# Even layer of a hybrid decoder: gates projected as [column, token], values of two heads per weight unit, softmax denominators and value copies through DRAM

## The chip, the cores and the metric

The kernel runs on one core of a Trainium2 chip. The time is device microseconds (us) of one execution; the median of several runs is the figure compared. The engines are named as in the profile: PE (TensorE matmul), PEld (its weight loads), DVE (VectorE), ACT (ScalarE), POOL (GpSimd) and SP (SyncE, which here only issues DMAs; all DMAs of this kernel are issued by SP, on one queue).

## The reference

A decoder trunk of two layers on x of 1024 tokens by 1024 channels: `h = h + even_mixer(norm(h))`, `h = h + odd_mixer(norm(h))`, then a final norm. The change touches only the even layer:

```python
def even_mixer(hn, w_in, w_out, lb, hgrn_norm_w):
    aq, ak, av, ag, bq, bf, bi, bg = split(hn @ w_in, [1024] * 8)
    a_out = dilated_mixture_attention(aq, ak, av)     # 16 heads of 64, windows (128,1) (512,4) (2048,16)
    b_out = hgrn2_chunked(bq, bf, bi, lb, hgrn_norm_w)  # 8 heads of 128, gated linear recurrence, RMS norm per head
    mixed = concatenate([a_out * silu(ag), b_out * silu(bg)], axis=-1)
    return mixed @ w_out
```

Each of the eight slices of the input projection has 1024 columns. `av` and `bi` are the values of the two head groups, `ag` and `bg` their gates. The attention output of a head is a sum over three dilated windows divided by one common denominator per token and head; the kernel multiplies the sum by the reciprocal of that denominator and by silu of the gate.

## The kernel before, in words

Matrix products are float32 products split into a high and a low part, three matmuls each (`mm3`, lines 147 to 151, so lines 148, 149 and 150 in the profile). The weights of the input projection come in units of 256 columns by 1024 rows, 4 DMAs of 256 KB each (`raww`); ACT rounds each piece to the high part (`w_hi`, line 113) and DVE subtracts for the low part (`w_lo`, line 114). One unit is loaded ahead (`unit`, line 136).

A unit is used in one of two ways:

- `proj_cols` (line 226) takes 128 of its columns as the stationary operand and streams 512 tokens: output [column, token], two halves of 8 x 3 matmuls of 512.
- `proj_toks` (line 241) takes 128 tokens as the stationary operand and streams the unit's 256 columns: output [token, column], eight blocks of 8 x 3 matmuls of 256.

Both are generators that hand back control after 6 matmuls of 512 or 12 of 256, each step counted as 1.3; `mix` (line 153) takes such steps as filling between the pieces of another generator.

Stage 1 (HGRN): for each of 8 heads `hgrn_chain(b)` runs, filled with the projections of the next head, `hgrn_in(b + 1)`: q and f by `proj_cols` (names bq, bf), then value and gate together by `proj_toks` (bi). Near the end of the chain POOL multiplies gate, norm and output (lines 524, 525), PE transposes the output (bt, line 531), ACT writes it to `y` and SP stores it to `ymix` in DRAM.

Stage 2 (attention): for each of 8 pairs of heads (called p) `attn(p)` runs, filled with `attn_in(p + 1)`: value and gate by `proj_toks` (av), q and k by `proj_cols` (aq, ak). PE's order is the written one here; ACT's, POOL's and SP's orders, and DVE's, are set by the planner. In `attn(p)`, eight blocks of 128 queries: `scores` (lines 587, 592) into two PSUM banks of tag "a" (there are two), DVE adds the window counts and takes the maximum (596), ACT takes exponents and sums the denominator `den` (601), `turn` lets DVE transpose 32x32 blocks into `PB` (607), and `near` and `distant` (621, 633) multiply with the values. Queries are held in the order (c a): partition 32a + c holds token 4c + a of its block. The values are needed replicated over the four residues a: `blocks` (557) copies them from SBUF to SBUF, 16 DMAs of 64 KB for half the tokens (`V<-v`, 564), and 4 of 96 KB for the far keys (`VF<-v`, 571).

The denominators go back to token order in `weigh` (636): 4 small DMAs, a reciprocal on DVE, and POOL multiplies the gate by it (645). `write` (647) transposes the weighed gate on PE (`gt`, 8 transposes into two banks "a", line 653), ACT halves it into `y`, DVE multiplies with the attention sums (657) and SP stores `y`. Both are called in the next head's `attn`: `weigh(p - 1)` after the scores of block 0, `write(p - 1)` in block 1. The last two blocks' products of head p - 1 (`rest`) are also done there.

Stage 3: in `attn(7)` the fill is the first four groups of the output projection, `out_first(range(4))` (names op, hres), with y read back from `ymix` (`rawy`, cut by the same lines 113 and 114 into yphi and yplo). In this part DVE's order is the written one too. The residual tiles `hres` take buffers of the tags X0, X1, v and sg.

Of the kernel before, what the change touches and what calls it, by code (L numbers as in the profile page):

```python
# [19 lines left out]
P = 128  # L20
# [16 lines left out]
C_LV = C_MA + 128  # L37
C_ID32 = C_LV + 5 * 16
C_T0 = C_ID32 + 32
C_ALL = C_T0 + 512  # L40


def const_table():
    c = np.zeros((P, C_ALL), np.float32)
    p = np.arange(P)
    c[:, C_ID:C_ID + 128] = np.eye(P)

    a, q = p // 32, p % 32 * 4 + p // 32

    def count(dist):  # L50
        cnt = np.zeros(dist.shape, np.int64)
        for window, dil in ((128, 1), (512, 4), (2048, 16)):
# [12 lines left out]
    for lv in range(5):  # L65
        s = 1 << lv
        blk = j // s
        i = np.arange(32)
        odd = i[(i // s) % 2 == 1]
        c[:, C_LV + 16 * lv:C_LV + 16 * lv + 16] = (blk[:, None] % 2 == 0) & (blk[:, None] + 1 == odd[None, :] // s)  # L70
    c[:, C_ID32:C_ID32 + 32] = j[:, None] == np.arange(32)[None, :]

    i, j = np.arange(32)[:, None], np.arange(16)[None, :]
    for par in range(2):
        c[(p // 16) % 2 == par, C_T0:C_T0 + 512] = (i == 2 * j + par).reshape(-1)
    return c


@with_exitstack
def trunk_kernel(ctx: ExitStack, tc: tile.TileContext, x, ew, ewo, ow, owab, owo, nw, fnw, lbl, hnw,  # L80
# [11 lines left out]
    def bank(tag, shape, name):  # L92
        return pp.tile(shape, F32, name=name, tag=tag, bufs=BANKS[tag])
# [226 lines left out]
    def even_layer(es):  # L320
        ep = es.enter_context(tc.tile_pool(name="ev", bufs=2))
        sm = es.enter_context(tc.tile_pool(name="evs", bufs=2))

        BIGS = {"X0": 2, "X1": 2, "v": 2, "sg": 3, "y": 2}
        HGS = {"q": 2, "f": 2, "AT": 2, "tot": 2, "osb": 2, "kn": 1, "S": 1, "nwb": 1, "x": 2}
        WAY = {"nwb": 1, "yh": 2, "yl": 2, "xn": 2, "h4": 1, "h5": 1, "h6": 1, "h7": 1}
        pool_of = {}
# [59 lines left out]
        nc.sync.dma_start(id32, cst[:, C_ID32:C_ID32 + 32])  # L387
        hw = sm.tile([P, 1], F32, name="hw", bufs=1)
        nc.sync.dma_start(hw, hnw)
        def hgrn_in(b):  # L390
            w = unit()
# [10 lines left out]
            for half in range(2):  # L402
                yield from proj_cols(w, 0, f"bq{b}", lambda s, ps: act.copy(q[:, s], ps), (half,))
                yield from proj_cols(w, 1, f"bf{b}", ev_f, (half,))
            dve.tensor_scalar(f, f, lb1[:, b:b + 1], lb[:, b:b + 1], op0=ALU.mult, op1=ALU.add)
            dve.tensor_scalar(kt, kt, lb1[:, b:b + 1], None, op0=ALU.mult)
            dve.tensor_tensor(qt, q, f, op=ALU.mult)
            w = unit()
            v = big("v", f"bv{b}", (P, NT, 128))
            sg = big("sg", f"bsg{b}", (P, NT, 128))  # L410
            INS[b] += [v, sg]

            def ev_v(t, ps):
                act.copy(v[:, t, :], ps[:, 0:128])
                act.activation(sg[:, t, :], ps[:, 128:256], AF.Sigmoid)
                dve.tensor_tensor(sg[:, t, :], ps[:, 128:256], sg[:, t, :], op=ALU.mult)

            yield from proj_toks(w, f"bi{b}", ev_v)

        INS = {}  # L420

        def hgrn_chain(b):
            q, qt, kt, f, v, sg = INS[b]
# [97 lines left out]
            act.activation(sd, ss, AF.Sqrt, bias=epsc, scale=1.0 / 128)  # L521
            rs = sm.tile([P, NT], F32, name=f"brs{b}", tag="brs")
            dve.reciprocal(rs, sd)
            pool.tensor_tensor(sg, sg, rs[:, :, None].to_broadcast([P, NT, 128]), op=ALU.mult)
            pool.tensor_tensor(osb, osb, sg, op=ALU.mult)
            yield 7.0
            y = big("y", f"by{b}")
            for h in range(2):
                tp = bank("d", [P, 512], f"bt{b}_{h}")
                for c in range(4):  # L530
                    pe.transpose(tp[:, c * 128:(c + 1) * 128], osb[:, 4 * h + c, :], ident)
                act.activation(y[:, h * 512:h * 512 + 512], tp, AF.Copy, scale=hw)
            nc.sync.dma_start(ymix[D + b * 128:D + (b + 1) * 128, :], y)

        def attn_in(p):
            w = unit()
            v = big("v", f"v{p}", (P, NT, 128))  # L540
            sg = big("sg", f"sg{p}", (P, NT, 128))
            INS[p] = [v, sg]

            def ev_v(t, ps):
                dve.tensor_copy(v[:, t, :], ps[:, 0:128])
                th = sm.tile([P, 128], F32, name=f"th{p}_{t}", tag="th")
                act.activation(th, ps[:, 128:256], AF.Tanh, scale=0.5)
                dve.scalar_tensor_tensor(sg[:, t, :], th, 1.0, ps[:, 128:256], op0=ALU.add, op1=ALU.mult)

            yield from proj_toks(w, f"av{p}", ev_v)  # L550
            w = unit()
            q, k = big("X0", f"aq{p}"), big("X1", f"ak{p}")
            INS[p] += [q, k]
            yield from proj_cols(w, 0, f"aq{p}", lambda s, ps: act.copy(q[:, s], ps))
            yield from proj_cols(w, 1, f"ak{p}", lambda s, ps: dve.tensor_copy(k[:, s], ps))

        def blocks(p, h):

            v = INS[p][0]

            V4 = at.tile([P, 4, NT // 2, 128], F32, name=f"V4{h}_{p}", tag=f"V4{h}")
            for b in range(4):
                for a in range(4):
                    nc.sync.dma_start(V4[32 * a:32 * a + 32, b], v[32 * b:32 * b + 32, NT // 2 * h:NT // 2 * h + NT // 2, :])
            VB.setdefault(p, []).append(V4)
            if h:

                VF = at.tile([P, NFAR, 128], F32, name=f"VF{p}", tag="VF")
                vr = v.rearrange("(c a) t d -> a c t d", a=4)
                for a in range(4):  # L570
                    nc.sync.dma_start(VF[32 * a:32 * a + 32], vr[a, :, 0:NFAR, :])
                VB[p].append(VF)

        def scores(p, i, den):

            q, k = INS[p][2:]
# [58 lines left out]

        def weigh(p):

            sg, den = INS[p][1], DEN[p]
            rd = sm.tile([P, NT, 2], F32, name=f"rd{p}", tag="rd")
            rv = rd.rearrange("(c a) t e -> a c t e", a=4)  # L640
            for a in range(4):
                nc.sync.dma_start(rv[a], den[32 * a:32 * a + 32])
            dve.reciprocal(rd, rd)
            g = sg.rearrange("p t (e d) -> p t e d", e=2)
            pool.tensor_tensor(g, g, rd[:, :, :, None].to_broadcast([P, NT, 2, 64]), op=ALU.mult)

        def write(p):
            sg, o = INS[p][1], O[p]
            y = big("y", f"ay{p}")
            for h in range(2):  # L650
                tp = bank("a", [P, 512], f"gt{p}_{h}")
                for t in range(4):
                    pe.transpose(tp[:, t * 128:(t + 1) * 128], sg[:, 4 * h + t, :], ident)
# [5 lines left out]

        def attn(p):  # L660

            DEN[p] = den = sm.tile([P, NT, 2], F32, name=f"den{p}", tag="den")
            if not p:
                blocks(0, 0)
            for i in range(NT):
                if i == 2:
# [22 lines left out]
        DEN, O, VB = {}, {}, {}  # L689


        h, h2, ready, asked = [], [], [4, 5, 6, 7, 0, 1, 2, 3], set()
# [42 lines left out]
        at = open_stage("at")  # L735
        G = at.tile([P, WG], F32, name="G")
        nc.sync.dma_start(G, cst[:, C_G:C_G + WG])
        PB = at.tile([P, 2, NT * WG + 192], F32, name="PB")
        with tc.manual_schedule(engines={mybir.EngineType.PE}):
            for p in range(7):  # L740
# [495 lines left out]
def host_layout(a):  # L1236
# [4 lines left out]
    for s in r128:  # L1241
        cols += [[np.r_[2048 + s, 3072 + s]], [s, 1024 + s]]
    for s in r128:
        cols += [[4096 + s, 5120 + s], [np.r_[6144 + s, 7168 + s]]]

    def unit(w, c):

# [51 lines left out]
```

## Time and profile before

| | |
|---|---|
| median of 3 runs | 2289.87 us (2287.13 to 2292.92) |
| the profiled execution, time | 2288.19 us |
| its span in the profile | 2286.4 us, 54636 instructions |
| granted TensorE clock, mean | 0.992 |
| PE busy | 2168.5 us, 95% of the span |
| DVE, ACT, POOL busy | 1427.2, 963.2, 227.7 us |
| first and last score matmul of the attention | 547.3 and 1051.7 us |

A row of the timeline gives the start in us from the span's start, the duration, the engine, the line of the kernel, the operation, what it writes and reads, shapes and a count; in square brackets stands the engine's idle time before it and what ended it. Rows of one kind that follow each other are merged with the count behind the x. PE overlaps its matmuls, so the pace of a stream is the distance between starts, not the duration.

### The profile page before, as it was taken

What the parts mean: (1) busy time and instruction counts of PE and PEld (TensorE: products, weight loads), DVE (VectorE), ACT (ScalarE), POOL (GpSimd) and SP (SyncE); (2) the same over time, 40 slices, a digit from 0 to 9 for tenths busy, and PEclk for the clock granted to TensorE, in tenths of its full rate; (3) what the DMA queues carried; (4) which work ended last, traced back from release to release, by engine and by line L of the source; (5) the groups of instructions that cost most, each with busy time, mean ns of one, the idle gap of its engine ahead of it and who ended that gap; (6) DMA issues with size and microseconds to landing.
All of it is one profiled execution on the core that took longest, in us unless ns stands there. A gap on an engine that the chain in (4) does not pass through costs nothing. (4 is left out here: it accounts for less than half of the span.)

```text
span 2286.4 us, 54636 instructions
## 1 busy us (share of the span) xinstructions
PE 2168.5 (95%) x22597; PEld 1806.7 (79%) x22597; DVE 1427.2 (62%) x3364; ACT 963.2 (42%) x2623; POOL 227.7 (10%) x236
## 2 busy tenths in 40 slices
PE   7999999999999999979999988989998989899998
PEld 6888888898888888857887776767777767678787
DVE  6444444444444444456677887878788877855777
ACT  5333333333323332322236663755555555544223
POOL 0000000000000000000000012131212121210000
PEclk9999999999999999989999999999999999999999
DMA  4111111113222323342234221121212121214232
GB/s 145 38 48 48 48 44 48 43 39 95 79 80 83 90 83 92 97 150 86 90 121 106 60 56 61 53 79 45 77 42 77 51 75 59 65 61 148 92 112 110
DMA packets 101864, 175.83 MB, mean 77 GB/s; under 512 B 16752, under 2 KB 34032, under 8 KB 101616
## 3 DMA queue, kind: packets, MB, share of 16 engines
q1 hardware_dynamic: 101616, 172.35, 24.3%
q8 instruction: 177, 2.90, 0.5%
q14 instruction: 71, 0.58, 0.1%
HBM read 127.07 MB, written 25.23 MB: 67 GB/s over the span
## 5 line engine op out<-in xcount | busy, mean ns | idle before, releaser
L114 DVE TENSOR_TENSOR w_lo<-raww,w_hi 128x512 fp32r<-128x512 f32 x292 | 212.1, 727 | 147.6 <-ACT w_hi L113 144.7
L113 ACT CAST w_hi<-raww 128x512 fp32r<-128x512 f32 x292 | 181.0, 620 | 265.7 <-DMA raww<-in_ewo_dram 52.7
L148 PE MATMUL av<-w_hi,hn_hi 128*128 128x256 f32 x512 | 149.1, 291 | 0.0
L148 PE MATMUL bi<-w_hi,hn_hi 128*128 128x256 f32 x512 | 147.0, 287 | 0.0
L149 PE MATMUL bi<-w_lo,hn_hi 128*128 128x256 f32 x512 | 145.4, 284 | 0.0
L150 PE MATMUL bi<-w_hi,hn_lo 128*128 128x256 f32 x512 | 144.9, 283 | 0.0
L149 PE MATMUL av<-w_lo,hn_hi 128*128 128x256 f32 x512 | 144.8, 283 | 0.0
L150 PE MATMUL av<-w_hi,hn_lo 128*128 128x256 f32 x512 | 144.6, 282 | 0.0
L601 ACT ACTIVATE P<-P,nm 128x256 f32<-128x256 f32 (+7 forms) x128 | 71.4, 559 | 130.2 <-DVE nm L599 126.8
L148 PE MATMUL op<-w_hi,yplo 128*128 128x512 f32 x288 | 113.9, 396 | 2.4 <-DVE hres L293 1.6
L150 PE MATMUL op<-w_hi,yplo 128*128 128x512 f32 x288 | 112.3, 390 | 0.0
L149 PE MATMUL op<-w_lo,yplo 128*128 128x512 f32 x288 | 112.2, 390 | 0.0
L148 PE MATMUL pv<-hn_hi,w_hi 128*128 128x512 f32 x256 | 107.2, 419 | 2.9 <-ACT uv L849 2.9
L148 PE MATMUL oz<-hn_hi,w_hi 128*128 128x512 f32 x256 | 109.3, 427 | 0.0
L293 DVE TENSOR_TENSOR hr<-hr,op 128x512 f32<-128x512 f32 x128 | 86.2, 684 | 33.7 <-PE op L150 33.5
L150 PE MATMUL pv<-hn_hi,w_lo 128*128 128x512 f32 x256 | 104.3, 408 | 0.0
L149 PE MATMUL pv<-hn_lo,w_hi 128*128 128x512 f32 x256 | 102.8, 402 | 0.0
L149 PE MATMUL oz<-hn_lo,w_hi 128*128 128x512 f32 x256 | 102.1, 399 | 0.0
L150 PE MATMUL oz<-hn_hi,w_lo 128*128 128x512 f32 x256 | 101.7, 397 | 0.0
L148 PEld LDWEIGHTS av<-w_hi,hn_hi 128*128 128x128 f32 x512 | 97.7, 191 | 3.5 <-issue 1.9
L148 PEld LDWEIGHTS bi<-w_hi,hn_hi 128*128 128x128 f32 x512 | 98.1, 192 | 0.0
L149 PEld LDWEIGHTS bi<-w_lo,hn_hi 128*128 128x128 f32 x512 | 98.1, 192 | 0.0
(354 smaller groups left out, 5994.4 us busy)
## 6 DMA issues: line engine op xcount, KB each, us to landing
raww<-in_ew_dram SPq DMA_DIRECT2D x128, 256.0 KB, 3.1
raww<-in_ow_dram SPq DMA_DIRECT2D x100, 256.0 KB, 3.0
V<-v SPq DMA_DIRECT2D x256, 64.0 KB, 2.0
rawy<-ymix SPq DMA_DIRECT2D x64, 256.0 KB, 2.7
raww<-in_ewo_dram SPq DMA_DIRECT2D x32, 256.0 KB, 3.0
gcl<-gcd SPq DMA_DIRECT2D x64, 128.0 KB, 3.0
gca<-gcd SPq DMA_DIRECT2D x64, 128.0 KB, 3.0
ymix<-oy SPq DMA_DIRECT2D x32, 256.0 KB, 2.1
```

The source lines that it names most:

```text
L113: act.copy(hi, raw)
L114: dve.tensor_tensor(lo, raw, hi.bitcast(F32), op=ALU.subtract)
L148: pe.matmul(ps, lh, rh, start=start, stop=False)
L149: pe.matmul(ps, lh, rl, start=False, stop=False)
L150: pe.matmul(ps, ll, rh, start=False, stop=stop)
L293: dve.tensor_tensor(dst[:, n], src[:, n], ps, op=ALU.add)
L601: act.activation(Pm[:, e, w0:], Pm[:, e, w0:], AF.Exp, bias=nmx[:, e:e + 1], scale=0.125, accum_out=den[:, i, e:e + 1])
```

## The change

Weights are regrouped: for two neighbouring blocks of 128 columns, s and z (two HGRN heads, or two of the attention's head pairs p), there are again four units, [v s | v z], [q s | k s], [gate s | q z], [k z | gate z] in the attention, and [q s | f s], [v s | v z], [gate s | q z], [f z | gate z] in HGRN. Values of two heads come from one `proj_toks`; gates come from `proj_cols`, so they are [column, token].

- HGRN: POOL multiplies the output by the norm before the transposes, and `y` by the gate after them.
- `blocks(p, 0)` stores the values of p to DRAM once (`vd`), and the copies are read from there, 4 DMAs in place of 16 for each half, and 4 for the far keys as before.
- The reciprocal is taken at the end of `attn(p)` on DVE. `weigh(p - 1)`, now called before the scores of block 0, brings it to token order and to rows with one matmul against a permutation matrix of halves (`PM`), into a bank "a"; ACT copies it out, SP stores it to DRAM (`rdd`) and loads it back into `y`, each row read by 64 partitions; POOL multiplies by the gate. `write` no longer transposes.
- Buffers: tag v 2 to 3, tag sg 3 to 2.

```diff
-        BIGS = {"X0": 2, "X1": 2, "v": 2, "sg": 3, "y": 2}
+        BIGS = {"X0": 2, "X1": 2, "v": 3, "sg": 2, "y": 2}
...
+        def values(b, name, copies):
+            w = unit()
+            V[b], V[b + 1] = (big("v", f"{name}{i}", (P, NT, 128)) for i in (b, b + 1))
+            def ev(t, ps):
+                for i in range(2):
+                    copies[i](V[b + i][:, t, :], ps[:, i * 128:i * 128 + 128])
+            yield from proj_toks(w, f"{name}p{b}", ev)
...
+            w = unit()
+            if b % 2 == 0:
+                for half in range(2):
+                    yield from proj_cols(w, 0, f"bq{b}", ev_q, (half,))
+                    yield from proj_cols(w, 1, f"bf{b}", ev_f, (half,))
+                rest()
+                yield from values(b, "bi", (act.copy, act.copy))
+            else:
+                yield from gate(w, 0, b - 1)
+                yield from proj_cols(w, 1, f"bq{b}", ev_q)
+                w = unit()
+                yield from proj_cols(w, 0, f"bf{b}", ev_f)
+                rest()
+                yield from gate(w, 1, b)
...
-            pool.tensor_tensor(sg, sg, rs[:, :, None].to_broadcast([P, NT, 128]), op=ALU.mult)
-            pool.tensor_tensor(osb, osb, sg, op=ALU.mult)
+            pool.tensor_tensor(osb, osb, rs[:, :, None].to_broadcast([P, NT, 128]), op=ALU.mult)
...
+                pool.tensor_tensor(y[:, h * 512:h * 512 + 512], y[:, h * 512:h * 512 + 512], SG[b][:, h * 512:h * 512 + 512],
+                                   op=ALU.mult)
...
+            if p % 2 == 0:
+                yield from values(p, "av", (dve.tensor_copy, act.copy))
+                w = unit()
+                yield from proj_cols(w, 0, f"aq{p}", ev_q)
+                yield from proj_cols(w, 1, f"ak{p}", ev_k)
+            else:
+                w = unit()
+                yield from gate(w, 0, p - 1)
+                yield from proj_cols(w, 1, f"aq{p}", ev_q)
+                w = unit()
+                yield from proj_cols(w, 0, f"ak{p}", ev_k)
+                yield from gate(w, 1, p)
...
-            for b in range(4):
-                for a in range(4):
-                    nc.sync.dma_start(V4[32 * a:32 * a + 32, b], v[32 * b:32 * b + 32, NT // 2 * h:NT // 2 * h + NT // 2, :])
+            if not h:
+                VD[p] = dp.tile([P, T], F32, name=f"vd{p}")
+                nc.sync.dma_start(VD[p], V[p].rearrange("p t d -> p (t d)"))
+            vd = VD[p]
+            for a in range(4):
+                nc.sync.dma_start(V4[32 * a:32 * a + 32].rearrange("p b t d -> p b (t d)"),
+                                  bass.AP(tensor=vd.tensor, offset=vd.offset + 512 * h, ap=[[T, 32], [32 * T, 4], [1, 512]]))
...
-            for a in range(4):
-                nc.sync.dma_start(rv[a], den[32 * a:32 * a + 32])
-            dve.reciprocal(rd, rd)
-            g = sg.rearrange("p t (e d) -> p t e d", e=2)
-            pool.tensor_tensor(g, g, rd[:, :, :, None].to_broadcast([P, NT, 2, 64]), op=ALU.mult)
+            rd = RD[p]
+            rp = bank("a", [2 * NT, 128], f"rp{p}")
+            pe.matmul(rp, rd.rearrange("p e t -> p (e t)"), PM, start=True, stop=True)
+            rs = sm.tile([2 * NT, 128], F32, name=f"rs_{p}", tag="rs_")
+            act.copy(rs, rp)
+            rdd = dp.tile([2 * NT, 128], F32, name=f"rdd{p}")
+            nc.sync.dma_start(rdd, rs)
+            y = Y[p] = big("y", f"ay{p}")
+            for e in range(2):
+                nc.sync.dma_start(y[64 * e:64 * e + 64], bass.AP(tensor=rdd.tensor, offset=rdd.offset + e * T, ap=[[0, 64], [1, T]]))
+            for h in range(2):
+                n = slice(512 * h, 512 * h + 512)
+                pool.tensor_tensor(y[:, n], y[:, n], SG[p][:, n], op=ALU.mult)
...
-            for h in range(2):
-                tp = bank("a", [P, 512], f"gt{p}_{h}")
-                for t in range(4):
-                    pe.transpose(tp[:, t * 128:(t + 1) * 128], sg[:, 4 * h + t, :], ident)
-                act.mul(y[:, h * 512:h * 512 + 512], tp, 0.5)
...
-            if not p:
+            if p:
+                weigh(p - 1)
+            else:
                 blocks(0, 0)
...
-                if i == 0 and p:
-                    weigh(p - 1)
...
+                if i == NT - 1:
+                    rd = RD[p] = sm.tile([P, 2, NT], F32, name=f"rd{p}", tag="rd")
+                    dve.reciprocal(rd.rearrange("p e t -> p t e"), den)
```

More of the change, by code (lines that the diff above doesn't have):

```diff
@@ L39 @@
 C_T0 = C_ID32 + 32
-C_ALL = C_T0 + 512
+C_PM = C_T0 + 512
+C_ALL = C_PM + 128
 def const_table():
@@ L400, in ev_f @@
                 act.activation(kt[:, s], ps, AF.Sigmoid, scale=-1.0)
[L402 to L407, printed above, removed]
@@ L408, in hgrn_in, with ev_q @@
-            w = unit()
[L409 to L420, printed above, removed]
+            def ev_q(s, ps):
+                act.copy(q[:, s], ps)
@@ new lines, in rest, with gate, ev @@
+            def rest():
+                dve.tensor_scalar(f, f, lb1[:, b:b + 1], lb[:, b:b + 1], op0=ALU.mult, op1=ALU.add)
+                dve.tensor_scalar(kt, kt, lb1[:, b:b + 1], None, op0=ALU.mult)
+                dve.tensor_tensor(qt, q, f, op=ALU.mult)
+            def gate(w, c, i):
+                sg = SG[i] = big("sg", f"bsg{i}")
+                def ev(s, ps):
+                    act.activation(sg[:, s], ps, AF.Sigmoid)
+                    dve.tensor_tensor(sg[:, s], ps, sg[:, s], op=ALU.mult)
+                yield from proj_cols(w, c, f"bg{i}", ev)
@@ L422, in hgrn_chain @@
+        INS, V, SG = {}, {}, {}
         def hgrn_chain(b):
-            q, qt, kt, f, v, sg = INS[b]
+            (q, qt, kt, f), v = INS[b], V[b]
             AT = big("AT", f"AT{b}", (P, NT, 128))
@@ L544, in ev_v @@
[L544 to L551, printed above, removed]
-            q, k = big("X0", f"aq{p}"), big("X1", f"ak{p}")
-            INS[p] += [q, k]
@@ L554, in attn_in, with ev_q, ev_k, gate @@
-            yield from proj_cols(w, 0, f"aq{p}", lambda s, ps: act.copy(q[:, s], ps))
-            yield from proj_cols(w, 1, f"ak{p}", lambda s, ps: dve.tensor_copy(k[:, s], ps))
+            q, k = big("X0", f"aq{p}"), big("X1", f"ak{p}")
+            INS[p] = [q, k]
+            def ev_q(s, ps):
+                act.copy(q[:, s], ps)
+            def ev_k(s, ps):
+                dve.tensor_copy(k[:, s], ps)
+            def gate(w, c, i):
+                sg = SG[i] = big("sg", f"sg{i}")
+                def ev(s, ps):
+                    act.activation(sg[:, s], ps, AF.Tanh, scale=0.5)
+                    dve.scalar_tensor_tensor(sg[:, s], sg[:, s], 1.0, ps, op0=ALU.add, op1=ALU.mult)
+                yield from proj_cols(w, c, f"ag{i}", ev)
@@ L636, in weigh @@
         def weigh(p):
-            sg, den = INS[p][1], DEN[p]
-            rd = sm.tile([P, NT, 2], F32, name=f"rd{p}", tag="rd")
-            rv = rd.rearrange("(c a) t e -> a c t e", a=4)
-            for a in range(4):
-                nc.sync.dma_start(rv[a], den[32 * a:32 * a + 32])
-            dve.reciprocal(rd, rd)
-            g = sg.rearrange("p t (e d) -> p t e d", e=2)
-            pool.tensor_tensor(g, g, rd[:, :, :, None].to_broadcast([P, NT, 2, 64]), op=ALU.mult)
-        def write(p):
-            sg, o = INS[p][1], O[p]
-            y = big("y", f"ay{p}")
-            for h in range(2):
-                tp = bank("a", [P, 512], f"gt{p}_{h}")
-                for t in range(4):
-                    pe.transpose(tp[:, t * 128:(t + 1) * 128], sg[:, 4 * h + t, :], ident)
-                act.mul(y[:, h * 512:h * 512 + 512], tp, 0.5)
+            rd = RD[p]
[11 more added lines that the diff above has]
+                pool.tensor_tensor(y[:, n], y[:, n], SG[p][:, n], op=ALU.mult)
+        def write(p):
+            y, o = Y[p], O[p]
             yv = y.rearrange("p (t c a) -> p a t c", c=32, a=4)
@@ L660, in attn @@
         def attn(p):
-            DEN[p] = den = sm.tile([P, NT, 2], F32, name=f"den{p}", tag="den")
-            if not p:
+            den = sm.tile([P, NT, 2], F32, name=f"den{p}", tag="den")
+            if p:
+                weigh(p - 1)
+            else:
                 blocks(0, 0)
@@ L737, in even_layer @@
         nc.sync.dma_start(G, cst[:, C_G:C_G + WG])
+        PM = at.tile([P, 128], F32, name="PM")
+        nc.sync.dma_start(PM, cst[:, C_PM:C_PM + 128])
         PB = at.tile([P, 2, NT * WG + 192], F32, name="PB")
@@ L1240, in host_layout @@
     cols = []
[L1241 to L1244, printed above, removed]
+    for s, z in zip(r128[::2], r128[1::2]):
+        cols += [[np.r_[2048 + s, 2048 + z]], [s, 1024 + s], [3072 + s, z], [1024 + z, 3072 + z]]
+    for s, z in zip(r128[::2], r128[1::2]):
+        cols += [[4096 + s, 5120 + s], [np.r_[6144 + s, 6144 + z]], [7168 + s, 4096 + z], [5120 + z, 7168 + z]]
     def unit(w, c):
```

15 lines of the change are left out of this document (5 added, 10 removed).

## The prediction

> **What bounds the kernel now.** I read the page first, then a table of windows of 60 us, then what PE waited for in each stage.
>
> ```profile
> span 2286.4 us, 54636 instructions
> PE 2168.5 (95%) x22597; PEld 1806.7 (79%) x22597; DVE 1427.2 (62%) x3364; ACT 963.2 (42%) x2623; POOL 227.7 (10%) x236
> 120.00:180.00 60.00, 59.69 (x790) 52.93 (x789) 26.07 (x56) 22.41 (x61) 5.43 (x5) 1.00 0.14 46
> 840.00:900.00 60.00, 60.00 (x1117) 51.28 (x1116) 28.64 (x78) 17.03 (x48) 1.90 (x1) 1.00 0.29 84
> 960.00:1020.00 60.00, 44.68 (x766) 34.08 (x765) 26.11 (x59) 15.46 (x38) 2.08 (x1) 0.86 0.46 144
> PE lp L451 <- DVE bkt L477: 5.1, 8, 1.6
> PE o L621 <- DVE PB L607: 11.3, 1, 11.3
> ```
>
> PE is the bound in both stages that the change touches: 59.69 of 60 us in HGRN (120 to 180), 60 of 60 in the attention (840 to 900), DVE and ACT below half. The one hole lies at 960 to 1020, where the last attention round begins: one wait of 11.3 us, and a mean clock of 0.86. In HGRN the largest wait sums to 5.1 us in 8. So only PE's own work, new waits of PE, and that hole count; evacuations, gates and POOL products lie under PE.
>
> **Projections.** Per two column blocks there were two `proj_toks` (384 matmuls of 256) and four `proj_cols` passes; now one and six: 192 matmuls of 256 are replaced by 96 of 512. Weight bytes, units and filling steps (32 a round) stay. A matmul's price is the distance of starts.
>
> ```profile
> 231.02 0.28 PE L150 MATMUL bi<-w_hi,hn_lo 128*128 128x256 f32 x1
> ...
> 238.82 0.28 PE L149 MATMUL bi<-w_lo,hn_hi 128*128 128x256 f32 x1
> ...
> 208.08 0.40 PE L150 MATMUL bq<-hn_hi,w_lo 128*128 128x512 f32 x1
> ...
> 210.14 0.39 PE L150 MATMUL bq<-hn_hi,w_lo 128*128 128x512 f32 x1
> ...
> 664.77 0.39 PE L148 MATMUL ak<-hn_hi,w_hi 128*128 128x512 f32 x1
> ...
> 668.62 0.39 PE L150 MATMUL ak<-hn_hi,w_lo 128*128 128x512 f32 x1
> ```
>
> 256 columns: 7.80 us over 65 steps, 0.120 us. 512 columns: 2.06 over 9, 0.229 us, in HGRN; 3.85 over 17, 0.2265 us, in the attention. A 512 saves 0.011 or 0.0135 us against two 256. Times 96 and four times a stage: 4.2 + 5.2 = 9.4 us less. The fence's durations (0.28 against 0.39) would promise far more, but they overlap. The Trainium skill, page "TensorE: Matmul & The Clock Gate", section "Back-to-back issue gap", gives a warm gap of N/2.4 + 2.5 ns: 109 and 216 ns, so only 2.4 ns a pair. By it this term would be an estimated 96 x 8 x 2.4 ns = 1.9 us and my sum 7.5 us smaller. The trace has 120 ns for 256, so the measurement decides.
>
> **Gate transposes.** `write` loses its 8 transposes.
>
> ```profile
> 618.93 0.28 PE L150 MATMUL av<-w_hi,hn_lo 128*128 128x256 f32 x1
> 619.05 1.04 PE L653 MATMUL gt<-ident,sg 128*128 128x128 f32 x8
> 619.84 0.36 PE L148 MATMUL av<-w_hi,hn_hi 128*128 128x256 f32 x1
> 620.04 0.28 PE L149 MATMUL av<-w_lo,hn_hi 128*128 128x256 f32 x1
> ```
>
> They hold the stream for 0.79 us, and the next matmul takes 0.20 instead of 0.12: 0.87 us a round, 8 rounds, 7.0 us less. ACT's two copies out of them go too, under PE.
>
> **The reciprocal's matmul.** It comes first in `attn(p)` for p = 1 to 7 and takes one of two banks "a"; the first score matmul takes the other, the second needs the first bank again, so PE waits until ACT has copied it out. Behind it on PE stand the scores, `rest` and all filling, so the wait counts in full. No such wait exists before; these rows bound it.
>
> ```profile
> 665.50 1.11 DVE L607 STREAM_TRANSPOSE PB<-P 128x896 f32<-128x896 f32 x1 [1.54 <-ACT P L601]
> ...
> 668.82 0.62 ACT L113 CAST w_hi<-raww 128x512 fp32r<-128x512 f32 x1 [2.10 <-PE ak L149]
> 668.94 0.48 PE L587 MATMUL S<-ak,aq 64*32 64x128 f32 x16
> ...
> 227.20 0.39 PE L512 MATMUL bops<-bv,AT 128*128 128x128 f32 x2
> ...
> 674.78 0.28 ACT L547 ACTIVATE th<-av 128x128 f32<-128x128 f32 x1 [0.69 <-DVE v L545]
> ...
> 538.03 0.60 PE L531 MATMUL bt<-ident,bo 128*128 128x128 f32 x4
> 538.66 0.69 ACT L532 ACTIVATE by<-bt,hw 128x512 f32<-128x512 f32 x1 [2.28 <-PE bt L531]
> 539.41 0.65 PE L531 MATMUL bt<-ident,bo 128*128 128x128 f32 x4
> ```
>
> The last three show such a handoff of one bank: ACT starts 0.03 us after PE's end, PE 0.06 after ACT's. Here: matmul from 668.94 (in the scores' place) for 0.39 us, ACT busy with a cast until 669.44, a copy of 128 columns 0.28, handoff 0.06: scores from 669.78, 0.84 us late. Where the filling ends with a gate (`attn_in` of odd p, ahead of four of the seven rounds) ACT first has that gate's second half, about 0.6 us more: 1.5 us. Sum 3 x 0.84 + 4 x 1.5 + 0.4 for the last `weigh` = 8.9 us more. Lower end 0.4 us each (the matmul alone), 3 us in all; upper end below, with the rivals. The reciprocal itself I take as ready: it follows `turn(7)`, which in this round ended at 666.61, 2.3 us before 668.94.
>
> **The hole at 1001.**
>
> ```profile
> 983.20 0.81 SPq L703 DMA_DIRECT2D hres<-in_x_dram  x2
> ...
> 992.07 10.74 SPq L564 DMA_DIRECT2D V<-v  x16
> 1002.91 2.44 SPq L571 DMA_DIRECT2D VF<-v  x4
> 1005.45 4.42 SPq L112 DMA_DIRECT2D rawy<-ymix  x3
> ...
> 1008.18 0.62 ACT L113 CAST yphi<-rawy 128x512 fp32r<-128x512 f32 x1 [10.01 <-DMA rawy<-ymix]
> 1011.48 0.71 DVE L607 STREAM_TRANSPOSE PB<-P 128x512 f32<-128x512 f32 x1
> 1012.24 1.29 PE L621 MATMUL o<-PB,V 32*64 32x64 f32 x64 [11.28 <-DVE PB L607]
> ...
> 986.00:988.00 2.00, 1.36 (x108) 1.22 (x109) 1.85 (x1) 0.00 (x0) 1.30 (x1) 1.00 1.00 396
> 1006.00:1008.00 2.00, 0.00 (x0) 0.00 (x0) 0.00 (x0) 0.00 (x0) 0.00 (x0) 0.50 0.75 255
> 1014.00:1016.00 2.00, 2.00 (x6) 1.55 (x5) 0.88 (x5) 0.99 (x4) 0.00 (x0) 0.50 0.33 111
> ```
>
> PE waits for `turn`, but that is DVE in written order: it stands behind the subtraction of yphi, that behind ACT's cast, that behind the load rawy, and SP issues this only after 16 V and 4 VF copies, 992.07 to 1005.35, 13.3 us. Eight DMAs replace these twenty. At 0.41 us each (hres, two in 0.81) they take 3.3 us to issue; their 1.75 MB at the 396 GB/s of 986 to 988 take 4.4 us, plus the 2.7 us that rawy took from issue to cast (1005.45 to 1008.18): a cast at 992.1 + 4.4 + 2.7 = 999.2. Against it, the store and two loads of `weigh(6)` now stand on SP ahead of it, and the residual's fourth tile takes a gate buffer that is free only after POOL's product: I allow 1 us, so 1000.2 and 8 us less idle. The clock is at 0.50 in the hole and for 3.8 us of work behind it (to 1016), which costs 1.9 us; a hole of 3 us may still lower it, so I count 1 us. Ends: 0, if SP is held elsewhere, and 11.3 + 1.9 us.
>
> **SP's waits.** Each round SP now waits for a store to DRAM before it can read it back, twice (values, reciprocals), with weight and rawy loads queued behind.
>
> ```profile
> ymix<-by SPq DMA_DIRECT2D x8, 512.0 KB, 2.6
> rawy<-ymix SPq DMA_DIRECT2D x64, 256.0 KB, 2.7
> ```
>
> A store takes 2.6 us to land, a load 2.7: about 5.3 us from copy-out to `y`, used one block later; V copies are needed some blocks later still, and weights are a unit ahead. I cost this at nothing while `attn_in` fills. If the cover is gone, each wait costs at most its 2.6 us. In the last round, where y's parts come just in time, I count 1.5 us more (0 to 5). The Trainium skill, page "DMA: Bandwidth & Descriptors", section "Anatomy of one DMA — SWDGE (gpsimd) path", puts a fixed 2.0 us on each DMA, mostly the write receipt; the trace's 2.6 us for 512 KB bears it out, and by it each readback waits about as I count.
>
> **At nothing**: HGRN's POOL products (moved behind the transposes; only the store of `y` follows), fewer and wider evacuations, the buffer counts (values of two blocks live beside one in use: three; gates of two blocks: two). Planner orders of later stages may shift by some us either way; in the range only.
>
> **Sum**: -9.4 - 7.0 + 8.9 - 8 - 1 + 1.5 = -15.0. From the profiled execution's 2288.19 us (span 2286.4 and 1.8 around it): 2273.2. That execution lay 1.7 under the median of the runs, so the median after is 2275 us.
>
> **Rivals.**
>
> 1. *The head of a round waits longer* (the slower side). If DVE does the reciprocal after the last w_lo, that waits for ACT's cast (to 669.44), so 0.7 us for w_lo, 0.25 for the reciprocal, then 0.39 + 0.28 + 0.06: 671.2, 2.2 us late, and up to 3.8 where POOL's work slows w_lo as at 533.25 (rows below this list; the reciprocal's 0.25 at 670.27). Without this term the sum is -23.9. From (23.9 - 6.9)/7 = 2.4 us a round it is no change, from (23.9 + 6.9)/7 = 4.4 us slower; at 5 us, 2290 + 11 = 2301. For it: the bank is really needed again at once. Against: `turn(7)` is long over, and the cast already waits for PE.
> 2. *The hole stays*: SP's V loads still wait, or rawy still lands late behind them. -15 + 9 = -6: 2284, no change. For it: the same loads, the same bytes, in the same place. Against: the 16 copies moved 1 MB in 10.74 us, 98 GB/s, where the same engines reached 396, so what held them was their issue.
> 3. *The paces even out*: if a stream of 512 in the new gates runs at 0.240 us, as two of 256, the 9.4 us are gone: 2284. Against: every 512 stream quoted runs at 0.23.
>
> ```profile
> 533.25 2.22 DVE L114 TENSOR_TENSOR w_lo<-raww,w_hi 128x512 fp32r<-128x512 f32 x1 [0.31 <-ACT w_hi L113]
> ...
> 670.27 0.25 DVE L643 RECIPROCAL rd<-rd 128x16 f32<-128x16 f32 x1 [2.82 <-DMA rd<-den]
> ```
>
> **How the numbers follow.** No change means within 0.3%, 6.9 us, about what a measurement of this kernel can tell. Forecast 0.62; rival 1 0.20 (0.08 of it slower, 0.12 no change); rival 2 0.14 (0.06 still faster, if half the hole closes); rival 3 0.04 (half each). Faster 0.62 + 0.06 + 0.02 = 0.70, same 0.12 + 0.08 + 0.02 = 0.22, slower 0.08. The range: all good ends (matmul alone -6, hole and clock -4, SP -1.5) give 2263; upward it takes in rival 2 and the no-change half of rival 1: 2260 to 2293. The forecast's own: 2263 to 2283.
>
> **What would show it.** Right: the distance between 512 starts stays at 0.23 and an HGRN round shrinks by 0.5 us; no gt; each round's first score matmuls 0.8 to 1.5 us later after the filling's last matmul, with PE waiting for ACT's copy; the wait before the first `near` of the last round at some 3 us. Wrong: PE waiting for the reciprocal (rival 1), an 11 us wait left (rival 2), or new waits of PE for weights or `near`'s values, which would mean that SP's readbacks are not covered.

## The result and the profile after

The changed kernel takes 2271.31 us (median of 4 runs, 2268.25 to 2272.7) against 2288.98 us before (4 runs): a ratio of 0.9919, 95% interval 0.9901 to 0.9936, so 17.7 us less, where 15 were forecast. The profiled execution took 2270.35 us, its span is 2268.6.

In what follows, a row of windows gives the window in us, its length, the busy time (and instructions) of PE, PEld, DVE, ACT and POOL, the granted clock, the time of the DMA packets as a share of 16 engines (it can exceed 1), and GB/s. A row of waits gives who waited for whom, the total in us, how often, and the longest. A row of one tile's matmuls gives their shortest, median and longest duration in ns and their first and last start.

The page of the changed kernel, the window of the table by 60 us in which the hole lay, and what PE waited for in HGRN (60 to 540 us), in the attention rounds (540 to 960) and in the last round (960 to 1080):

```profile
span 2268.6 us, 52553 instructions
PE 2162.0 (95%) x21781; PEld 1760.6 (78%) x21781; DVE 1409.7 (62%) x3236; ACT 950.0 (42%) x2551; POOL 239.5 (11%) x252
```

```profile
960.00:1020.00 60.00, 50.65 (x781) 37.97 (x780) 31.81 (x70) 16.91 (x44) 2.95 (x2) 0.89 0.52 153
```

```profile
PE lp L479 <- DVE bkt L505: 1.6, 3, 0.9
PE S L633 <- ACT rs L688: 1.3, 3, 0.4
PE op L151 <- DVE hres L296: 5.4, 3, 3.9
PE op L151 <- ACT yphi L116: 4.3, 1, 4.3
PE o L667 <- issue: 1.0, 1, 1.0
```

PE is as full as before. HGRN's wait for bkt shrank from 5.1 us in eight to 1.6 in three, which was not forecast; the rounds have the new wait for ACT's copy `rs`; and the single wait of 11.3 us is gone, but two of 4 us (hres, yphi) stand in its place.

Where the time came from can be read from three marks that both kernels have: the first score matmul, the first `near` that PE runs in the last round (it still belongs to head 6), the last score matmul. The score matmuls of the changed kernel, and the two rows of its last round's head:

```profile
L633 PE MATMUL S<-ak,aq x1024: 269/376/639, 540.0 to 1036.0; 64*32 64x256 f32 x150, 64*32 64x128 f32 x21
```

```profile
972.24 0.39 PE L686 MATMUL rp<-PM,rd 128*16 128x128 f32 x2
...
973.54 0.72 PE L667 MATMUL o<-PB,V 32*64 32x64 f32 x41
```

And the same mark of the kernel before:

```profile
983.73 0.86 PE L621 MATMUL o<-PB,V 32*64 32x64 f32 x60
```

| stretch | before | after | difference | forecast |
|---|---|---|---|---|
| to the first score (HGRN) | 547.3 | 540.0 | -7.3 | -4.2 |
| to the last round's first near | 436.4 | 433.5 | -2.9 | -1.9 |
| to the last score | 68.0 | 62.5 | -5.5 | -8.4 |
| to the end | 1234.7 | 1232.6 | -2.1 | -0.5 |

The forecast column is the prediction's own terms put to these stretches (a round's transposes at -0.87, the reciprocals' matmuls at +8.9 in all). The total came out near because two errors of some 3 us, in the first and the third stretch, had opposite signs; that is luck. Kernels with the same HGRN code (this one, and the third to seventh below) have their first score between 538.1 and 540.0, so the first stretch is known to about 1 us either way. The last stretch is known less well: these kernels, whose code there is the same, need 1232.6 to 1238.3 us for it, so its -2.1 is not clear of the spread.

### The profile page after: what moved, and what is told of

It is laid out like the page before. It is cut to its first block, busy times and chain, and to the rows that moved or that the text cites. A ratio compares the mean times of both kernels' runs of the same rounds, so it can differ in the third digit from the quotient of the medians.

```text
span 2268.6 us, 52553 instructions
## 1 busy us (share of the span) xinstructions
PE 2162.0 (95%) x21781; PEld 1760.6 (78%) x21781; DVE 1409.7 (62%) x3236; ACT 950.0 (42%) x2551; POOL 239.5 (11%) x252
## 5 line engine op out<-in xcount | busy, mean ns | idle before, releaser
L653 DVE STREAM_TRANSPOSE PB<-P 128x256 f32<-128x256 f32 (+3 forms) x64 | 54.6, 853 | 72.8 <-ACT P L647 72.8
L1156 POOL TENSOR_TENSOR gca<-gca,MA 128x256 f32<-128x256 f32 x64 | 50.6, 791 | 453.8 <-DMA gca<-gcd 252.8
L296 DVE TENSOR_TENSOR hres<-hres,op 128x512 f32<-128x512 f32 x96 | 64.7, 682 | 31.8 <-PE op L153 29.4
L642 DVE CUSTOM_DVE_ANT_0 P<-S,G 128x256 f32<-128x256 f32 (+7 forms) x128 | 58.2, 492 | 36.8 <-PE S L638 35.2
L904 DVE SCALAR_TENSOR_TENSOR vT<-uv,cws,vT 128x512 f32<-128x512 f32 x96 | 74.3, 774 | 4.7 <-ACT vT L902 3.8
L1084 DVE TENSOR_TENSOR tm<-Lp,Tp 128x126 f32<-128x126 f32 (+22 forms) x248 | 74.9, 302 | 3.7
L1158 ACT ACTIVATE gca<-gca,g_ngc 128x128 f32<-128x128 f32 x128 | 45.8, 401 | 69.3 <-POOL gca L1156 69.1
L151 PE MATMUL avp<-w_hi,hn_hi 128*128 128x256 f32 x256 | 74.5, 291 | 0.0
L151 PE MATMUL op<-w_hi,yphi 128*128 128x512 f32 x160 | 65.9, 412 | 8.5 <-ACT yphi L116 4.6
```

Of the source, the lines that this page charges most:

```text
L151: pe.matmul(ps, lh, rh, start=start, stop=False)
L296: dve.tensor_tensor(dst[:, n], src[:, n], ps, op=ALU.add)
L642: dve.tensor_tensor_reduce(Pm[:, e, w0:], S[e][:, w0:WG], G[:, w0:], 1.0, -3e38, op0=ALU.add, op1=ALU.max, accum_out=mx[:, e:e + 1])
L653: dve.transpose(PB[:, :, i * WG + w0:(i + 1) * WG], Pm[:, :, w0:])
L904: dve.scalar_tensor_tensor(a[0][:, s], ub[:, i + s.start:i + s.stop], cws[:, tile_no, i:i + 1], a[0][:, s], op0=ALU.mult, op1=ALU.add)
L1084: dve.tensor_tensor(tm[:, :31 - k, :n], Lp[:, k, k + 1:, None].to_broadcast([P, 31 - k, n]), Tp[:, k:k + 1, :n].to_broadcast([P, 31 - k, n ...
```

## The experiments

All are timed against the kernel before, which took 2290.68, 2290.26 and 2289.65 us in the three groups; ratios carry their 95% intervals.

**Each half alone.** HGRN of the change with the attention of before, and the other way round:

```diff
 # e1: hgrn_in, hgrn_chain, HGRN's unit columns from the change
-            v = big("v", f"v{p}", (P, NT, 128))
-            sg = big("sg", f"sg{p}", (P, NT, 128))
+            v = big("sg", f"v{p}", (P, NT, 128))
+            sg = big("v", f"sg{p}", (P, NT, 128))
 # e2: attn_in, blocks, weigh, write, attn, its unit columns from the change
-            v = big("v", f"bv{b}", (P, NT, 128))
-            sg = big("sg", f"bsg{b}", (P, NT, 128))
+            v = big("sg", f"bv{b}", (P, NT, 128))
+            sg = big("v", f"bsg{b}", (P, NT, 128))
```

> Only the HGRN half of the change; the attention is that of before (its value and gate tiles swap the two buffer tags, so that the tags' sizes are those of the change). Theory: the gain of HGRN stands by itself, 96 x 8 matmuls' worth of pace there (4.2 us) and 3.5 us less of PE waiting for DVE's bkt: about -7.5 us against before, 2281.5; the profile shows the wait lp <- bkt near 1.6 us in place of 5.1 and the first score matmul near 540 us in place of 547. Rival: the pace alone, -4 us (2285), the waits being a matter of the planner's order; second rival: no gain without the attention half, 2289.

> Only the attention half; HGRN is that of before (its value and gate tiles swap the two buffer tags). Theory: -10 us against before, 2279: about -4.5 in the rounds (pace -5.2, transposes gone -5.2, the reciprocal's bank wait +5.8), -5 in the last round, -1 behind it. Rival: the halves share a gain (order of later stages), then this gives clearly more or less than 17.7 minus what the HGRN half alone gives.

HGRN alone: 2282.41 us, 0.9967 (0.9955 to 0.9978), 7.6 us less. Attention alone: 2279.14 us, 0.9949 (0.9935 to 0.9962), 11.7 us less. Together 19.3, against the 18.6 that 0.9919 makes of the same base: the halves add up. PE's waits for bkt in HGRN, first of the HGRN half, then of the attention half (whose HGRN is the old one):

```profile
PE lp L476 <- DVE bkt L502: 1.3, 4, 0.4
```

```profile
PE lp L465 <- DVE bkt L491: 4.6, 8, 1.2
```

The waits for bkt go with the HGRN half and stay with the old HGRN: 3.3 to 3.8 us of shorter waits leave some 4 of the 7.6 for the pace, whose forecast was 4.2. The first score of the HGRN half comes at 539.0 us. The rival of the pace alone is out.

**The value copies.** `blocks` taken from the kernel before, all else as changed:

```diff
-            for a in range(4):
-                nc.sync.dma_start(V4[32 * a:32 * a + 32]..., bass.AP(tensor=vd.tensor, ...))
+            for b in range(4):
+                for a in range(4):
+                    nc.sync.dma_start(V4[32 * a:32 * a + 32, b], v[32 * b:32 * b + 32, NT // 2 * h:NT // 2 * h + NT // 2, :])
...
```

> The change, with the value copies taken from SBUF again (16 + 16 + 4 DMAs a round, no copy in DRAM). Theory: the twenty DMAs are what held SP and the yphi loads at the last round's start, so the 11 us wait of the first near comes back and the time is 4 to 8 us above the changed kernel, 2275 to 2279; the rounds before stay at 124.8 us a pair. Rival: what shortened the hole is the moved reciprocal and the loads' order on SP, not the copies: within 2 us of the changed kernel, 2271.

2278.36 us, 0.9939 (0.9924 to 0.9953): some 4.6 us of the gain gone by the ratios, whose intervals overlap, 7 by the medians. SP's rows, and PE's waits in the last round:

```profile
979.13 12.74 SPq L607 DMA_DIRECT2D V<-av  x16
991.97 2.45 SPq L614 DMA_DIRECT2D VF<-av  x4
994.51 1.00 SPq L115 DMA_DIRECT2D rawy<-ymix  x2
```

```profile
PE op L151 <- DVE hres L296: 11.0, 3, 9.4
PE op L151 <- ACT yphi L116: 4.8, 1, 4.8
```

The twenty copies hold SP for 15.3 us (13.3 in the kernel before), yphi's loads start at 994.5, and a wait of 9.4 us is back, in front of hres instead of near. From the first near of the last round (973.60) to the last score (1042.9) this kernel takes 69.3 us, the changed one 62.5; up to that near they agree within half a microsecond. So the copies through DRAM are worth 5 to 7 us, all of it in the last round.

**The reciprocal's bank.** One word changed:

```diff
-            rp = bank("a", [2 * NT, 128], f"rp{p}")
+            rp = bank("pj", [2 * NT, 128], f"rp{p}")
```

> The change, with the reciprocal's matmul in a projection bank (tag pj) in place of a score bank (tag a). Theory: the scores no longer wait for ACT's copy, so the gap from the matmul to the first near shrinks from 1.14 and 1.6 us to about 0.75, 3 x 0.4 + 4 x 0.85 = 4.6 us less: 2266.7 against 2271.3 for the change. Rival: the wait moves to the filling's first projection, which needs the pj bank that the last evacuation or the copy still holds: no gain, 2271.

2265.92 us, 0.9892 (0.9876 to 0.9908). Two heads of rounds in the changed kernel, one behind a gate's projection and one behind k's, then the first of them in this one:

```profile
597.36 0.39 PE L153 MATMUL ag<-hn_hi,w_lo 128*128 128x512 f32 x1
597.68 0.39 PE L686 MATMUL rp<-PM,rd 128*16 128x128 f32 x2
598.00 0.43 PE L633 MATMUL S<-ak,aq 64*32 64x128 f32 x2
598.87 0.48 PE L633 MATMUL S<-ak,aq 64*32 64x128 f32 x14 [0.43 <-ACT rs L688]
...
660.83 0.39 PE L686 MATMUL rp<-PM,rd 128*16 128x128 f32 x2
661.15 0.89 PE L633 MATMUL S<-ak,aq 64*32 64x128 f32 x16
661.97 0.85 PE L667 MATMUL o<-PB,V 32*64 32x64 f32 x60
```

```profile
595.83 0.39 PE L686 MATMUL rp<-PM,rd 128*16 128x128 f32 x2
596.15 0.48 PE L633 MATMUL S<-ak,aq 64*32 64x128 f32 x16
596.56 0.85 PE L667 MATMUL o<-PB,V 32*64 32x64 f32 x60
```

In the changed kernel two score matmuls run, the other fourteen wait for `rs`: from `rp` to the first near 1.14 us behind k (660.83 to 661.97) and, with the scores' 0.41 us added to 598.87, 1.6 us behind a gate. In the projection bank it is 0.73 (595.83 to 596.56). In the last round of the changed kernel it was 1.30 (972.24 to 973.54), so 3 x 0.41 + 3 x 0.87 + 0.57 = 4.4 us were to be had. 5.4 came by the medians (2271.31 to 2265.92); the intervals of the two ratios overlap, the rows decide for 4.4. In the rounds the wait did not move to the fill: from 540 to 950 us PE has no wait left. In the last round 0.7 us of it did (0.4 for the bank, which hres still held, 0.3 for `rs`).

**The transposes back.** Eight per round, as before, results unused:

```diff
         def write(p):
             y, o = Y[p], O[p]
+            for h in range(2):
+                tp = bank("a", [P, 512], f"gt{p}_{h}")
+                for t in range(4):
+                    pe.transpose(tp[:, t * 128:(t + 1) * 128], SG[p][:, (4 * h + t) * 128:(4 * h + t + 1) * 128], ident)
```

> The change, with 8 transposes a round put back into the score banks where they stood (their results are read by nobody). Theory: each round gets 0.87 us longer, 7.0 us in all: 2278. Rival: in the changed kernel PE has slack there (it waits for ACT or DVE anyway in each round), so they cost less than 3 us: below 2274.

2276.34 us, 0.9945 (0.9931 to 0.9959), 5.0 us above the change by the medians, 6.0 by the ratios, whose intervals overlap. The transposes and the heads of rounds 2 and 4 of this kernel:

```profile
611.50 1.04 PE L703 MATMUL gt<-ident,sg 128*128 128x128 f32 x8
...
661.28 0.39 PE L686 MATMUL rp<-PM,rd 128*16 128x128 f32 x2
...
787.97 0.39 PE L686 MATMUL rp<-PM,rd 128*16 128x128 f32 x2
```

Two rounds take 126.7 us here (787.97 - 661.28). In the changed kernel, whose fourth round has its head at 785.67, they take 124.84:

```profile
785.67 0.39 PE L686 MATMUL rp<-PM,rd 128*16 128x128 f32 x2
```

That is 0.92 us a round, against 0.87 forecast. Over all six rounds from the first head to the last (597.26 to 977.16, against 597.68 to 972.24) it is 0.89. The rival of slack in PE is out.

**What is left of the hole.** In the changed kernel the loads of SP, the two waits of PE, ACT and DVE ahead of the second wait, and windows of 2 us read:

```profile
976.95 1.09 SPq L693 DMA_DIRECT2D ay<-rdd  x2
...
979.47 2.35 SPq L609 DMA_DIRECT2D V<-vd  x4
981.92 4.68 SPq L616 DMA_DIRECT2D VF<-vd  x4
987.41 1.45 SPq L115 DMA_DIRECT2D rawy<-ymix  x2
```

```profile
983.79 0.79 PE L151 MATMUL op<-w_hi,yphi 128*128 128x512 f32 x1 [4.32 <-ACT yphi L116]
994.23 0.79 PE L151 MATMUL op<-w_hi,yphi 128*128 128x512 f32 x1 [3.85 <-DVE hres L296]
```

```profile
992.23 1.29 ACT L116 CAST yphi<-rawy 128x512 fp32r<-128x512 f32 x2 [5.13 <-DMA rawy<-ymix]
992.88 0.69 DVE L117 TENSOR_TENSOR yphi<-rawy,yphi 128x512 fp32r<-128x512 f32 x1 [6.37 <-ACT yphi L116]
993.49 0.68 DVE L296 TENSOR_TENSOR hres<-hres,op 128x512 f32<-128x512 f32 x1
```

```profile
984.00:986.00 2.00, 2.00 (x5) 1.35 (x6) 1.97 (x8) 0.00 (x0) 1.83 (x2) 0.50 1.04 194
986.00:988.00 2.00, 2.00 (x6) 1.51 (x6) 0.52 (x1) 1.09 (x4) 0.00 (x0) 0.50 1.08 231
...
998.00:1000.00 2.00, 2.00 (x89) 1.82 (x74) 2.00 (x7) 0.38 (x1) 0.00 (x0) 0.50 0.52 209
```

The eight copies leave SP in 7 us (979.47 to 986.60) where I had 3.3, and the DMA engines are full at 194 to 231 GB/s, half of the 396 that I had. The yphi loads start at 987.4, their cast comes at 992.2, and behind it stand DVE's subtraction, hres and PE. Two experiments took this apart. In one, each copy fills 128 partitions instead of 32 (with the same bytes and rows, but with other keys' rows, so the near products are wrong); in the other, on top of the projection bank, the copies are asked for two blocks later:

```diff
 # e5
-            for a in range(4):
-                nc.sync.dma_start(V4[32 * a:32 * a + 32]..., ap=[[T, 32], [32 * T, 4], [1, 512]])
+            for b in range(4):
+                nc.sync.dma_start(V4[:, b]..., ap=[[T, P], [1, 512]])
 # e6
-                if i == 1:
+                if i == (1 if p < 7 else 3):
                     blocks(p, 1)
```

> The change, with the V4 loads filling all 128 partitions each (same bytes, same size of row, same number of DMAs; each partition gets another key's row, so the near products use wrong values; only the time is of interest). The changed kernel moved 194 to 257 GB/s with its DMA engines fully busy while these loads ran, 396 was seen elsewhere. Theory: a load into only 32 partitions is what is slow; then these loads land in some 3 us instead of 5.3, the DMA share at the last round's start drops, the wait of 3.9 us behind them shrinks by 2 to 3 us, and the time is 2 to 4 us below the change, 2268 to 2269. Rival: the rate is that of reading back DRAM or of the traffic beside it; landing stays near 5 us and the time within 1 us of 2271.

> On top of the reciprocal in a projection bank: in the last round the second half of the V copies and the far keys are asked for in block 3 instead of block 1, so SP puts them behind the loads of yphi. Theory: those copies' 1.75 MB ahead of yphi are what is left of the hole; the wait of PE on hres at 990 us (3.3 us in that kernel) goes and the clock is not lowered a second time: 4 to 5 us less, 2261 to 2262 against 2265.9. Rival: the loads of the residual and of the reciprocals hold SP as well, or near then waits for its values: 0 to -1 us, 2265.

The wide rows: 2267.46 us, 0.9905 (0.9891 to 0.9918), 3.2 us under the change by the ratios, whose intervals overlap, so the times do not settle it. Two windows in a middle round, with the copies of the changed kernel and then with the wide ones:

```profile
612.00:614.00 2.00, 2.00 (x19) 2.00 (x19) 0.78 (x3) 0.27 (x1) 0.00 (x0) 1.00 1.09 240
614.00:616.00 2.00, 2.00 (x61) 1.73 (x63) 0.48 (x2) 0.27 (x1) 0.00 (x0) 1.00 1.01 254
```

```profile
610.00:612.00 2.00, 2.00 (x19) 2.00 (x19) 1.17 (x3) 0.27 (x1) 0.00 (x0) 1.00 0.98 306
612.00:614.00 2.00, 2.00 (x44) 1.75 (x42) 0.29 (x1) 0.27 (x1) 0.00 (x0) 1.00 1.02 312
```

With the engines as full, 306 to 312 GB/s in place of 240 to 254: the number of partitions is part of the rate, though not all of the distance to 396 (the far keys' loads kept their 32). The copies' median time to landing went from 5.3 to 4.0 us, where 3 was expected. The wait on hres shrank only from 3.9 to 3.1 us, not by the 2 to 3 expected, and the wait for yphi grew from 4.3 to 4.8.

The late copies: 2262.88 us, 0.9882 (0.9868 to 0.9895), 3 us under the kernel with the projection bank alone, again with overlapping intervals. Its waits in the last round:

```profile
PE op L151 <- ACT yphi L116: 3.7, 1, 3.7
...
PE op L151 <- DVE hres L296: 1.5, 2, 1.3
```

The wait behind the copies is gone (4.9 us in three to 1.5 in two), so they were its cause. The one ahead of them, 3.7 us for yphi, stays: it stands behind the reciprocals' readback and the residual's loads on SP. Those were not moved, so that they are its cause is not shown.

**The clock in the last round.** Waits are only part of what the last round costs; work at a granted clock of 0.50 is the other. For each kernel, from the first near of the last round to the last score: the time in which PE is idle, and the time lost to the clock, an estimate that takes half of PE's busy time at 0.50 (all in us of the profiled executions):

| kernel | stretch | PE idle | lost to the clock | clock at 0.50 |
|---|---|---|---|---|
| before | 68.0 | 15.3 | 4.4 | 990.4 to 993.8, 1004.1 to 1017.7 |
| changed | 62.5 | 9.2 | 6.0 | 983.1 to 989.9, 993.3 to 1000.1 |
| copies from SBUF | 69.3 | 15.2 | 6.9 | 981.6 to 988.4, 991.8 to 1008.9 |
| projection bank | 62.4 | 11.5 | 2.7 | 973.5 to 983.7 |
| wide rows | 59.0 | 9.6 | 1.6 | 980.9 to 984.4 |
| late copies, projection bank | 57.7 | 6.8 | 3.3 | 974.7 to 984.9 |

What is left of a stretch after both is 47.2 to 48.2 us in every row, so these two account for it. The change took 6.1 us from PE's idle time and lost 1.6 more to the clock. The wide rows did not shorten PE's idle time at all: their stretch is 3.5 us shorter because the clock fell once instead of twice. The late copies took 4.7 us of idle time from the kernel with the projection bank, more than the one wait of 3.3; but that kernel's clock had already fallen only once, so nothing was to be had there.

**The wide rows with the right keys**, on the change and on the fastest kernel:

```diff
-            for a in range(4):
-                nc.sync.dma_start(V4[32 * a:32 * a + 32]..., ap=[[T, 32], [32 * T, 4], [1, 512]])
+            for b in range(4):
+                nc.sync.dma_start(V4[:, b]..., bass.AP(tensor=vd.tensor, offset=vd.offset + 32 * b * T + 512 * h, ap=[[0, 4], [T, 32], [1, 512]]))
```

> The change, with each V4 load filling all 128 partitions with the right keys: one DMA for each quarter of a block, its source read four times over by a zero step outermost. Theory: as with the rows on 128 partitions before, 306 to 312 GB/s in place of 240 to 254 while such loads run, landing near 4.0 us, 3 to 4 us less than the change: 2267 to 2268. Rival, as the Trainium skill's page "DMA: Bandwidth & Descriptors", section "Rules for kernel authors", has it: an outermost dimension of 4 confines a DMA to at most 4 of the 16 engines; then each load takes about as long as four shares of it would, landing goes to 8 us or more, and the time is that of the change or above it, 2271 to 2276.

> The same loads on top of the late V copies and the reciprocal in a projection bank. Theory: where the copies already stand behind the loads of yphi their speed matters little: -0 to -2 us against 2262.9, 2261 to 2263. Rival (the four engines): 2263 to 2268.

2283.54 us, 0.9971 (0.996 to 0.9982), and 2275.96 us, 0.9939 (0.9927 to 0.9951): 12 to 13 us slower than the same kernels without it, worse than either theory had it. A window while these loads run on the change, one from the same place in the changed kernel itself, PE's longest wait with them between 530 and 950 us, which the change does not have, and its wait on hres in the last round:

```profile
546.00:548.00 2.00, 2.00 (x10) 1.64 (x9) 1.32 (x6) 0.61 (x3) 0.00 (x0) 1.00 0.26 102
```

```profile
544.00:546.00 2.00, 2.00 (x10) 1.45 (x8) 0.45 (x1) 0.12 (x2) 0.00 (x0) 1.00 1.07 218
```

```profile
PE S L633 <- DVE mx L642: 5.7, 1, 5.7
```

```profile
PE op L151 <- DVE hres L296: 12.2, 3, 10.6
```

The first wait is new, the second was 5.4: 12.5 us more, about the whole loss. The rows ahead of the first wait, which ends at 564.43:

```profile
539.36 8.84 SPq L609 DMA_DIRECT2D V<-vd  x4
552.22 3.64 SPq L115 DMA_DIRECT2D raww<-in_ew_dram  x2
562.07 0.62 ACT L116 CAST w_hi<-raww 128x512 fp32r<-128x512 f32 x1 [12.61 <-DMA raww<-in_ew_dram]
```

Four copies hold SP for 8.84 us (1.89 in the changed kernel), the weight load behind them goes out at 552.22 instead of 546.20, and ACT waits 12.6 us for it. In the order that the planner gave ACT here, this cast stands ahead of the gate and the next exponents (in the changed kernel behind them, at 563.00), so the maximum of the scores, and with it PE, waits too.

The rate is 102 GB/s, less than half of the 218 in the changed kernel. The Trainium skill, page "DMA: Bandwidth & Descriptors", section "Rules for kernel authors", says that an outermost dimension of 4 confines a DMA to at most 4 of the 16 engines. The trace agrees: a share of 0.26, where four full engines of sixteen make 0.25, against 1.07. The engines were not counted one by one.

## Why the prediction was right, and where its steps were off

- *What bounds it*: PE, its new waits and the hole. It held, but for the granted clock: in the last round that moved by as much as the waits (table above).
- *Projections, -9.4*: the pace of 512 stayed at 0.23 us (a gate's 24 matmuls start from 592.01 to 597.36), so rival 3 is out. (The formula cited in the prediction saves 2.5 ns a pair, not 2.4; the 1.9 us stands.) Missed was a part of HGRN: 3.5 us of waits for bkt went with it. I had listed these waits and then left them out, as a detail of DVE's order. In the kernel before, all eight rounds have such a wait, with two w_lo close ahead of the bkt product on DVE (252.09 and 254.23 us, for one); in the changed one the rounds at 79 and 196 us still have both, the round at 137 us has neither (131.41 and 134.83). That this order is the cause is read from the rows and was not tested; the two halves show that the waits go with the HGRN half.
- *Gate transposes, -7.0*: putting them back costs 0.89 to 0.92 us a round by the rows, so 7.1 to 7.4 in all; the times of that run give 5 to 6.
- *The reciprocal's matmul, +8.9*: the mechanism is the forecast one, the sizes 0.73 us (0.84 forecast) behind k, and 1.19 behind a gate (1.5; 0.89 in the last round), 6.6 over the seven heads. Rival 1 did not come: PE waited nowhere for the reciprocal.
- *The hole, -8 and -1 for the clock, +1.5 for SP*: -7.5 forecast, -4.6 measured (the -5.5 of the third stretch less 0.87 for a transpose). The clock is the term that failed: 1 us was to be won and 1.6 were lost, since the clock fell behind each of two holes. Before, too, it cost more than the 1.9 us read there: the work at 0.50 ran to 1017.7, and there was an earlier stretch from 990.4. The idle time came out by luck, 6.1 us less where -8 and +1.5 make 6.5, for its parts are others: the wait of 11.3 us for near is gone, waits of 3.9 for hres and 4.3 for yphi are new, and two small ones shrank. What delayed yphi, and hres behind it, is the term "1.75 MB at the 396 GB/s of 986 to 988", and both factors are wrong. Four loads of 256 KB and four of 96 KB are 1.44 MB. The rate came from loads that fill 128 partitions; the windows with copies into 32 show 194 to 254. So yphi's cast came 12.8 us after the copies' start (979.47 to 992.23) instead of 7.1: 7.9 to the issue of its load, where 4.4 was forecast, and 4.8 from there to the cast, where 2.7 was. Besides, the readback of the reciprocals and the residual's loads now split yphi's four loads, and PE waits 4.3 us for the fourth.
- *SP's waits at nothing*: right in the rounds, where PE waits for no value, no `y` and no weight (540 to 960 us: only `rs`, 1.3 us). The fixed 2.0 us on each DMA, cited in the prediction, is not borne out by the small ones: the store of the reciprocals, 8 KB, landed after 1.4 us (median), and before the change the loads of the denominators, 2 KB, after 1.7.

Rival 2, that the hole stays, was right by half: PE's idle time in the last round's stretch stayed at 9.2 of 15.3 us, and its second hole for the reason named there (the same loads in the same place).

## What to carry to other kernels

A PSUM bank taken out of a pool that the next matmuls need at once puts the round trip of its evacuation on PE, however small the matmul is (0.73 to 1.19 us a round here); one from a pool that is idle then costs the matmul alone (0.32 us, 595.83 to 596.15). One word was worth 4.4 us. When one DMA replaces many, count its bytes, take its rate from a load of the same shape, with as many partitions, not from the fastest row of the trace, and look at which loads it now stands ahead of. Small waits that a view lists may be a term of the sum: here 3.5 us, beside 4.2 for the pace. Where a kernel has holes, add up idle time and work at a lowered clock separately: a change can win the one and lose the other.

The fastest of the kernels run is the change with the reciprocal in a projection bank and the last round's copies asked for two blocks later: 2262.88 us, 0.9882 of the time before.

## What the runs showed of the hardware that I had not expected

- While loads into 32 partitions ran (2 KB a row, beside the far keys'), the DMA engines were full at 194 to 254 GB/s; with the same rows into 128 partitions, 306 to 312.
- A load with a zero step of 4 outermost on its source ran at 102 GB/s, with the DMA engines at a share of 0.26, and cost 12 to 13 us in the kernel.
- Each stretch at a clock of 0.50 in the table lasts 3.4 us or a multiple of it (6.8, 10.2, 13.7, 17.1). The length of a hole alone does not decide whether the clock falls. Behind holes of 3.1 us (wide rows) and 3.3 us (projection bank), each for hres, it stayed at 1.00. In the kernel with the projection bank it fell behind an earlier hole of only 2.3 us, and while PE was at work again:

```profile
972.10 0.60 PE L667 MATMUL o<-PB,V 32*64 32x32 f32 x37 [2.29 <-issue]
...
974.00:976.00 2.00, 1.05 (x3) 0.33 (x1) 0.69 (x1) 0.17 (x1) 0.00 (x0) 0.50 0.97 245
```

What does decide was not tested.
